# Layer 0 of a hybrid trunk: scale tiles loaded ahead of the shifts, half of the shifts taken as rows by VectorE

## The chip, the cores and the metric

The kernel runs on one core of a Trainium2 chip. The metric is the device time of one launch in microseconds. The engines are PE (TensorE, with its weight loads as PEld), DVE (VectorE), ACT (ScalarE), POOL (GpSimd) and SP (SyncE, which issues nearly all the DMAs here).

## The reference

A trunk of two layers runs over 128 context tokens and 512 latent tokens, 640 columns in all (`T`), with a width of 2048 (`D`), which is 16 tiles of 128 (`KT`). Context and latent tokens have a conditioning vector each (`c_ctx`, `c`), so every modulation is wanted twice. Cut to what matters:

```
shift, scale, gate = silu(cond) @ ada_w[l] + ada_b[l]          # three vectors of 2048
h = rms_norm(x, norm_g[l]) * (1 + scale) + shift
# layer 0 (even): qa ka va | qb kb vb rb | gp = h @ w_in        # rb: 32 rank columns, gp: 2048
y = concat(window_attention(...), gated_linear_attention(...)) * silu(gp)
# layer 1 (odd): neighbourhood attention | spatial-gating MLP, also * silu(gp)
x = x + gate * (y @ w_out[l])
```

After the two layers a final norm follows. Keys, values and scan states of the context are outputs too.

## The kernel before, in words

**Layout and projections.** Activations lie with the features on the partitions: 16 tiles of 128 x 640. Each projection (a "chunk" of 128 output features) runs over the 16 k-tiles in `mm_k` (L385), in two halves of 320 columns (`HT`). For fp32 accuracy each product is three matmuls: high part by high part, low part of the activation (`actl`, in the code `al`) by the high part of the weight, and high part of the activation (`acth`, `ah`) by the low part of the weight. One k of one chunk is so six matmuls. Weights come as `wraw` and are split by ACT (`whi`) and POOL (`wlo`); in the start the splits are called `suhi` and `sulo`.

**Modulation in a projection.** `act_mod` multiplies x by `A` = (1 + scale) * norm_g for one k-tile, and splits it. The norm's own factor (`rstd`) is applied when a sum leaves its bank. The shift can't be added there, so `ah` and `al` carry two more columns, the shift for context and for latent tokens; the first half of a chunk then has 322 columns, and those two come out as a bias. A chunk's third field in `add` says whether it takes these columns.

**The start (`start`).** Nothing of layer 0 can run before its scale and shift are there. `ada_w` of layer 0 comes as 16 tiles (f), each of 256 columns (128 of shift, 128 of scale) in four DMAs of 512 KB, through a ring of `NR` = 7 buffers (`Y` and `more`), beside three buffers for the tiles of x. For each quarter four fp32 matmuls of 32x256 run on four column groups of PE (L1311); ACT copies the sum, two matmuls with a selector (`sel`) turn it into columns, DVE makes `A` and the shift, and `act_mod` makes the tile. Two chunks (`LEAD`) follow tile by tile; the other six of the first eight (`FIRST`: six gates, the rank columns `w_rb` and the first query chunk) run in `WINDOWS` of k-tiles, each window summed into `YB` by DVE, the shift columns into `part_b`. The last window (k 12 to 15) is done behind the start by `finish`.

**Vectors that are taken as rows.** The gate vector of layer 0 and shift and scale of layer 1 are not made on PE. `ada_task` loads rows of the transposed weights (128 features x 512), and DVE multiplies each with the broadcast `silu(cond)` and sums along the row: one reduction for each of the two conditions, each with a read-out of the sum, into `part`. The jobs run one after another: `g0` (16 tiles), then `1` (32 tiles, shift first and scale behind it within each piece of 512 columns). They form a low-priority task (`self.low`) that yields to other work.

**Who sets the order.** A planner, `Pace`, keeps a modelled clock for each engine (`self.now`, `tick`) while the program is emitted, and each engine's order is what it emits. Chunks, evacuations, loads and the low task are emitted when the planner thinks them ready; loads go through SP's queue in the order of `dma`. A `need(flag)` keeps emission at a point until the flag is set: `need("ada_1")` (L2257) stands ahead of the handover from layer 0 to layer 1. The evacuation of an output pair makes two tiles of layer 1's x (bank times gate plus x, `OUT0` is their order); the handover scales these tiles by the new `A` and splits them while the last output pairs are still on PE, and PE's first chunks of layer 1 go k by k behind it.

## Time and profile before

| | |
|---|---|
| three runs | 2129.94, 2124.6, 2125.88 us; median 2125.88 us |
| profiled execution | 2124.6 us, of which the traced span is 2122.5 us |
| granted clock of PE, mean | 0.995 |
| busy share of the span | PE 97%, DVE 65%, POOL 52%, ACT 45% |
| DMA | 330.66 MB, mean 156 GB/s; 374 and 405 GB/s in the first two slices of 53 us |
| instructions | PE 14104, DVE 3235, ACT 2138, POOL 946 |

The busy share of PE counts pipelined matmuls whose ends are modelled, so 97% says that PE hardly ever waits, not that each of its matmuls is as short as it can be. Averages over the span say little about the two places that the change touches, the first 190 us and the end of layer 0 near 1040 us; both are read from stretches, waits and single instructions. In the rows a buffer is named by the program: `bank` is a PSUM bank, `adas` the four row buffers of `ada_task`, `more` and `Y` in the first 120 us the ring of modulation tiles.

### The profile page before, as it was taken

How to read it: one execution, taken by the hardware profiler on the slowest of the kernel's cores; microseconds unless marked ns; L12 is line 12 of the kernel's file. 1: busy time of each engine (PE TensorE's matmuls, PEld its weight loads, DVE VectorE, ACT ScalarE, POOL GpSimd, SP SyncE). 2: the span in 40 equal slices, each digit the busy share in tenths (PEclk: the TensorE clock that was granted, in tenths of full speed). 3: DMA queues.
4: the chain of work that ended last, by engine and by line, in shares of the span. 5: the costliest groups of instructions: out<-in, count | busy, mean ns of one | idle time of the engine just before them, and what ended most of it. 6: DMA issues, size and time to landing. Idle time of an engine off the chain costs nothing.

```text
span 2122.5 us, 39172 instructions
## 1 busy us (share of the span) xinstructions
PE 2064.9 (97%) x14104; PEld 1995.1 (94%) x14104; DVE 1378.1 (65%) x3235; ACT 945.2 (45%) x2138; POOL 1113.5 (52%) x946
## 2 busy tenths in 40 slices
PE   7999999999999999999999999999999999999996
PEld 4799999999989999999999999999999999999995
DVE  2437776777777875898766888777454444465335
ACT  3424444343333444543464444444444544454443
POOL 4333333223223223788665666555655577767883
PEclk9999999999999999999999999999999999999998
DMA  9925432345445335476843455443322344363337
GB/s 374 405 104 161 131 110 98 105 126 173 145 151 167 119 115 160 150 237 221 288 130 105 135 169 159 148 147 119 99 75 94 107 137 130 110 223 128 127 96 251
DMA packets 185283, 330.66 MB, mean 156 GB/s; under 512 B 20032, under 2 KB 69248, under 8 KB 185088
## 3 DMA queue, kind: packets, MB, share of 16 engines
q1 hardware_dynamic: 183616, 326.60, 46.9%
q8 instruction: 110, 1.80, 0.3%
q10 hardware_dynamic: 1472, 1.56, 0.2%
q14 instruction: 85, 0.70, 0.1%
HBM read 293.59 MB, written 31.87 MB: 153 GB/s over the span
## 4 chain that ended last, share of the span: by engine, by line
PE 86%; DVE 4%; DMA 3%; POOL 2%; ACT 2%; issue 2%; SPq 1%; ACTq 0%; DVEq 0%; POOLq 0%
PE bank L385 82%; PE bank L390 2%; POOL wlo L212 2%; PE bank L1311 1%; DVE arena L212 1%; DVE Y L212 1%; DVE adas L212 1%; DMA adas<-ada 1%; DMA wraw<-w_even 1%; SPq L418 1%; ACT whi L212 1%; POOL arena L212 0%; ACT arena L212 0%; DVE bank L212 0%; POOL actl L212 0%
## 5 line engine op out<-in xcount | busy, mean ns | idle before, releaser
L385 PE MATMUL bank<-acth,whi 128*128 128x320 f32 (+1 forms) x3296 | 1011.1, 318 | 7.4 <-DVE arena L212 2.8
L385 PE MATMUL bank<-actl,whi 128*128 128x320 f32 (+1 forms) x3296 | 985.8, 310 | 3.5 <-POOL actl L212 2.0
L385 PE MATMUL bank<-acth,wlo 128*128 128x320 f32 (+1 forms) x3296 | 985.9, 310 | 3.3 <-POOL wlo L212 3.2
L212 POOL TENSOR_TENSOR wlo<-wraw,whi 128x512 fp32r<-128x512 f32 (+1 forms) x449 | 571.4, 1284 | 646.8 <-ACT whi L212 565.2
L385 PEld LDWEIGHTS bank<-acth,whi 128*128 128x128 f32 x3296 | 611.5, 188 | 21.3 <-issue 4.9
L385 PEld LDWEIGHTS bank<-actl,whi 128*128 128x128 f32 x3296 | 611.5, 188 | 6.7 <-DMA actl<-bl_dram 2.8
L385 PEld LDWEIGHTS bank<-acth,wlo 128*128 128x128 f32 x3296 | 611.6, 188 | 5.2 <-POOL wlo L212 5.1
L212 POOL TENSOR_TENSOR wlo<-rs,whi 128x384 fp32r<-128x384 f32 x370 | 407.4, 1118 | 192.9 <-ACT whi L212 151.3
L212 ACT ACTIVATE whi<-wraw 128x512 fp32r<-128x512 f32 (+1 forms) x457 | 260.9, 588 | 148.6 <-PE bank L385 104.4
L385 PE MATMUL bank<-eh,whi 128*128 128x322 f32 (+1 forms) x666 | 209.4, 314 | 0.1
L385 PE MATMUL bank<-eh,wlo 128*128 128x322 f32 (+1 forms) x666 | 207.0, 311 | 1.7 <-POOL wlo L212 1.7
L385 PE MATMUL bank<-el,whi 128*128 128x322 f32 (+1 forms) x666 | 207.1, 311 | 0.0
L212 ACT ACTIVATE whi<-rs 128x384 fp32r<-128x384 f32 x370 | 181.6, 514 | 43.8 <-PE bank L385 35.3
L212 DVE CUSTOM_DVE_ANT_0 adas<-adas,bank,partg 128x256 bf16<-128x256 f32 (+1 forms) x320 | 178.4, 557 | 13.1 <-ACT bank L212 5.7
L212 DVE CUSTOM_DVE_ANT_0 adas<-adas,bank,part 128x512 bf16<-128x512 f32 x192 | 143.0, 745 | 18.2 <-ACT bank L212 6.9
L212 DVE TENSOR_TENSOR wraw<-rs 128x768 f32<-128x768 f32 x74 | 95.0, 1283 | 81.9 <-POOL wlo L212 49.8
L212 ACT ACTIVATE arena<-arena,bc 128x512 f32<-128x512 f32 (+4 forms) x211 | 106.0, 527 | 92.1 <-DVE arena L212 89.1
L212 DVE TENSOR_TENSOR bank<-bank,sums 128x320 f32<-128x320 f32 (+1 forms) x148 | 71.7, 495 | 100.7 <-PE bank L385 62.3
L385 PEld LDWEIGHTS bank<-eh,wlo 128*128 128x128 f32 x666 | 125.3, 188 | 2.8 <-POOL wlo L212 2.8
L385 PEld LDWEIGHTS bank<-eh,whi 128*128 128x128 f32 x666 | 125.7, 189 | 0.6 <-ACT whi L212 0.4
L385 PEld LDWEIGHTS bank<-el,whi 128*128 128x128 f32 x666 | 125.9, 189 | 0.0
L212 ACT ACTIVATE arena<-Y 128x320 f32<-128x320 f32 (+1 forms) x76 | 39.0, 513 | 154.7 <-DVE Y L212 127.0
(194 smaller groups left out, 2242.9 us busy)
## 6 DMA issues: line engine op xcount, KB each, us to landing
wraw<-w_even SPq DMA_DIRECT2D x176, 256.0 KB, 3.2
adas<-ada_g SPq DMA_DIRECT2D x128, 256.0 KB, 3.6
adas<-ada SPq DMA_DIRECT2D x128, 256.0 KB, 3.8
rs<-w_odd SPq DMA_DIRECT2D x50, 384.0 KB, 3.3
wraw<-w_odd SPq DMA_DIRECT2D x74, 256.0 KB, 3.6
more<-ada SPq DMA_DIRECT2D x36, 512.0 KB, 8.2
wraw<-w_out SPq DMA_DIRECT2D x64, 256.0 KB, 3.9
Y<-ada SPq DMA_DIRECT2D x28, 512.0 KB, 7.6
```

Source lines behind the costliest of these rows:

```text
L212: return f(*args, **kw)
L385: self.nc.tensor.matmul(out, lhsT, rhs, start=start, stop=stop, **kw)
L390: self.nc.tensor.transpose(out, in_, self.ident[:k, :k])
L418: self.nc.sync.dma_start(out, in_)
L1311: nc.tensor.matmul(o, c, w[:, j, :], start=(q == 0), stop=(q == 3))
```

## The change

Modulation of layer 0 is cut anew. `ada0` holds 24 tiles of 128 columns: first the 16 scale tiles, then the last eight shift tiles (`BOTH`), each in two DMAs of 512 KB. An activation tile needs only its scale, so it can be made ahead of the shifts. The first eight shift tiles are taken as rows (`shifts`): DVE reduces `ada_s0` against `silu(cond)`, which PE broadcasts into two banks by products with a one-hot matrix. The finished shift is written as columns into `ah` and `al`, and as rows into DRAM (`shift_s`).

The six gates of the start (`FIRST` is now 6) run before the shift is there, so they do without shift columns: 320 columns in place of 322, in windows of 2, 2, 4 and 8 k-tiles, summed in `yt(8 + c)`. What their shift columns would have given comes later as rows: a new job `b0` stands first in `ada_task`, which reduces the gates' weights (`gateT`) against the shift rows, and `gates0` then applies `rstd` (POOL) and SiLU with that bias (ACT). The rank chunk and the first query chunk become ordinary chunks behind the start. `finish`, with its last window, goes away, and `able` may take a window out of turn.

On **PE** the program begins so. `bank_71` holds the modulation sums, `bank_72` what the selector makes of them, `bank_67` to `bank_70` the first chunks. Before:

```order
L1311 MATMUL bank_71<-Y,cond_111 32x256 x12
L1311 MATMUL bank_71<-more_115,cond_111 32x256 x4
L385 MATMUL bank_72<-small,adas 128x2 x2
L1311 MATMUL bank_71<-more_115,cond_111 32x256 x8
L385 MATMUL bank_67<-acth,suhi_179 128x322
L385 MATMUL bank_68<-acth,suhi_179 128x320
L385 MATMUL bank_67<-actl,suhi_179 128x322
```

After:

```order
L1317 MATMUL bank_71<-Y,cond_112 32x128 x16
L386 MATMUL bank_72<-small,adas 128x2
L1317 MATMUL bank_71<-Y,cond_112 32x128 x8
L1317 MATMUL bank_71<-more_116,cond_112 32x128 x8
L386 MATMUL bank_67<-acth,suhi_156 128x320
L386 MATMUL bank_68<-acth,suhi_156 128x320
```

A tile is now 16 matmuls of 128 columns and one selector product, where it was 16 of 256 columns and two products; the first projection stands behind two tiles' worth of these matmuls, where it stood behind one and a half.

On **SP** the loads that stand at the same place are these. `wraw<-w_even` are weights of the first chunks, `Y<-xT` tiles of x. Before:

```order
L418 DMA Y<-ada 128x1024 x3
L418 DMA more_115<-ada 128x1024
L418 DMA Y<-xT 128x640
L418 DMA more_115<-ada 128x1024 x3
L418 DMA Y<-xT 128x640 x2
L418 DMA wraw<-w_even 128x512 x4
```

After, the first rows, and the place where the row loads come in (`raw` are their buffers, `ada_s` the transposed shift columns):

```order
L420 DMA Y<-ada 128x1024 x2
L420 DMA Y<-xT 128x640
L420 DMA wraw<-w_even 128x512
L420 DMA Y<-ada 128x1024
L420 DMA more_116<-ada 128x1024
```
```order
L420 DMA wraw<-w_even 128x512
L420 DMA raw_290<-crow_s 2x512
L420 DMA raw_291<-ada_s 128x512
L420 DMA raw_292<-ada_s 128x512
L420 DMA raw_293<-ada_s 128x512
L420 DMA raw_294<-ada_s 128x512
L420 DMA wraw<-w_even 128x512
L420 DMA Y<-ada 128x1024
```

The first weight load moved from behind seven pieces and three tiles of x to behind two pieces and one tile; row loads now stand among the scale pieces.

On **DVE**, at the end of layer 0, an `ISA` row is a reduction (two inputs) or its read-out (one), `bank_71` and `bank_67` or `bank_69` hold an output pair, and `A_95<-part` begins the scale of layer 1. Before:

```order
L212 ISA adas,part_103<-adas,bank_74,part_103 128x512
L212 ISA part_103 128x1
L212 TENSOR_TENSOR bank_71<-bank_71,sums_7739 128x320
L212 TENSOR_TENSOR bank_69<-bank_69,sums_7739 128x320
L212 SCALAR_TENSOR_TENSOR Y<-bank_69,G_96,arena_7743 128x128
L212 SCALAR_TENSOR_TENSOR Y<-bank_69,G_96,arena_7743 128x192
L212 SCALAR_TENSOR_TENSOR Y<-bank_71,G_96,arena_7743 128x320
L212 TENSOR_TENSOR A_95<-part_103,b_92 128x16
L212 TENSOR_TENSOR A_95<-A_95,small 128x16
```

After, where the line of dots stands for 22 more pairs of a reduction and its read-out, in two alternating banks:

```order
L213 TENSOR_TENSOR bank_71<-bank_71,sums_7907 128x320
L213 TENSOR_TENSOR bank_67<-bank_67,sums_7907 128x320
L213 SCALAR_TENSOR_TENSOR Y<-bank_67,G_96,arena_7911 128x128
L213 SCALAR_TENSOR_TENSOR Y<-bank_67,G_96,arena_7911 128x192
L213 SCALAR_TENSOR_TENSOR Y<-bank_71,G_96,arena_7911 128x320
L213 ISA adas,part_104<-adas,bank_73,part_104 128x512
L213 ISA part_104 128x1
...
L213 TENSOR_TENSOR A_95<-part_104,b_92 128x16
L213 TENSOR_TENSOR A_95<-A_95,small 128x16
```

Before, the last reduction stood ahead of this output pair's evacuation; now 24 reductions stand between the evacuation and `A_95`. The evacuation of the next output pair stands behind the whole scaling of layer 1's first tiles in both programs, and PE's first pair of layer 1 writes the banks of that output pair.

The core of the diff:

```diff
-WINDOWS = ((0, 2), (2, 2), (4, 4), (8, 4))
+WINDOWS = ((0, 2), (2, 2), (4, 4), (8, 8))
...
-LEAD, FIRST = 2, 8
+LEAD, FIRST = 1, 6
+BOTH = 8
...
+    lags0, room0, rows_at, pace0, NRAW, NRING = (0.2,) * 5, 1.2, 20.0, 0.4, 6, 6
...
+                    src = self.d["shift_s" if name == "b0" else "crow_s"]
+                    todo.append((fit, src[c : c + m, cs].partition_broadcast(128), bank[c : c + m]))
...
             def load(j):
-                if j < 4 * KT:
-                    self.dma(ring[j % NR], d["ada0"][j // 4, :, 4 * (j % 4) : 4 * (j % 4) + 4, :])
+                if j < 2 * (KT + BOTH):
+                    self.dma(ring[j % NR], d["ada0"][j])
...
             def tiles():
-                for f in range(KT):
-                    for q in range(4):
-                        w = ring[(4 * f + q) % NR]
+                for i in range(KT + BOTH):
+                    for q in range(2):
+                        w = ring[(2 * i + q) % NR].rearrange("p (a b) -> p a b", b=128)
                         yield from self.until(w)
-                        for j in range(4):
-                            o, c = pm[32 * j : 32 * j + 32, 0:256], cond[:, 4 * q + j, :]
-                            self.pe(0.15, o, c, w[:, j, :])
-                            nc.tensor.matmul(o, c, w[:, j, :], start=(q == 0), stop=(q == 3))
-                        load(4 * f + q + NR)
-                        if q % 2:
-                            yield
+                        for j in range(8):
+                            g = 32 * (j % 4)
+                            o, c = pm[g : g + 32, 0:128], cond[:, 8 * q + j, :]
+                            self.pe(0.075, o, c, w[:, j, :])
+                            nc.tensor.matmul(o, c, w[:, j, :], start=(q == 0 and j < 4), stop=(q == 1 and j >= 4))
+                        load(2 * i + q + NR)
+                        yield
                     r = rows.next()
-                    nc.scalar.activation(r, pm[:, 0:256], AF.Copy)
+                    nc.scalar.activation(r, pm[:, 0:128], AF.Copy)
                     yield from self.until(r)
                     p = pcol.next()
-                    self.mm(p[:, 0:2], r[:, 128:256], self.sel)
-                    self.mm(p[:, 2:4], r[:, 0:128], self.sel)
-                    nc.vector.tensor_scalar(
-                        self.A[0][:, f, :], p[:, 0:2], self.b1[:, 0, f : f + 1], self.ng[:, 0, f : f + 1], ALU.add, ALU.mult
-                    )
-                    sh = self.s("sh", 2)
-                    nc.vector.tensor_scalar(sh, p[:, 2:4], self.adab[:, 0, f : f + 1], None, ALU.add)
+                    self.mm(p, r, self.sel)
+                    f = i if i < KT else i - BOTH
+                    x = self.adab[:, 0, f : f + 1]
+                    if i >= KT:
+                        nc.vector.tensor_scalar(self.sh0[:, :, f], p, x, None, ALU.add)
+                        continue
+                    x, g = self.b1[:, 0, f : f + 1], self.ng[:, 0, f : f + 1]
+                    nc.vector.tensor_scalar(self.A[0][:, f, :], p, x, g, ALU.add, ALU.mult)
                     yield from self.wait(f"sq{f}")
                     self.act_mod(0, f, xs[f % NX], 0, T)
-                    nc.scalar.activation(self.ah[:, f, 0:2], sh, AF.Copy)
-                    nc.vector.tensor_tensor(self.al[:, f, 0:2], sh, self.ah[:, f, 0:2].bitcast(F32), ALU.subtract)
                     load_x(f + NX)
                     self.flags.add(f"act{f}")
+                self.flags.add("tiles")
...
+            def shifts():
+                raws = [self.t(su, [128, PIECE], "raw", bufs=self.NRAW) for _ in range(self.NRAW)]
+                junk = self.t(su, [128, PIECE // 2], "junk").bitcast(BF16)
+                one = self.t(su, [2, 2, 128], "one", F32R)
+                hi, lo = (self.t(su, [2, PIECE], x, F32R) for x in ("chi", "clo"))
+                nc.vector.tensor_copy(one, self.ident[0:2, 0:2, None].to_broadcast([2, 2, 128]))
+                pc = self.banks[2:4]
...
+                for q in range(4):
+                    cs = slice(PIECE * q, PIECE * q + PIECE)
+                    todo += [(None, d["crow_s"][:, cs]), *((f, d["ada_s0"][f, :, cs]) for f in range(NB))]
+                def load(i):
+                    if i < len(todo):
+                        x = raws[i % len(raws)]
+                        self.dma(x[0:2, :] if todo[i][0] is None else x, todo[i][1])
...
+                for i, (f, _) in enumerate(todo):
+                    raw = raws[i % len(raws)]
+                    if f is None:
...
+                        for c, p in enumerate(pc):
+                            self.mm(p, one[:, c, :], hi, stop=False)
+                            self.mm(p, one[:, c, :], lo, start=False)
+                        continue
...
+                        nc.vector.tensor_tensor_reduce(junk, raw, p, 1.0, acc if i > NB else 0.0, ALU.mult, ALU.add, acc)
+                        yield self.pace0
...
+                yield from self.wait("tiles")
+                self.shifts(self.ah[:, :, 0:2], self.al[:, :, 0:2], self.sh0.rearrange("p c f -> p f c"))
+                self.flags.add("shift0")
...
+                self.dma(d["shift_s"].rearrange("a (b c) -> (a b) c", c=128), crow)
+                self.flags.add("rows0")
...
-                M, y = self.chunks[c][1], self.ysum(c)
-                pieces = [(y[:M, 0:HT], pw[:M, 2 : 2 + HT]), (self.part_b[:M, c, :], pw[:M, 0:2])]
-                if half:
-                    pieces = [(y[:M, HT:T], pw[:M, 0:HT])]
-                for y, p in pieces:
-                    if k0 == 0:
-                        nc.scalar.activation(y, p, AF.Copy)
-                    else:
-                        nc.vector.tensor_tensor(y, y, p, ALU.add)
-            for j in range(4):
+                    if k % 2:
+                        self.tick(2)
+                y = self.yt(8 + c)[:, HT * half : HT * half + HT]
+                if k0 == 0:
+                    nc.scalar.activation(y, pw[:, 0:HT], AF.Copy)
+                else:
+                    nc.vector.tensor_tensor(y, y, pw[:, 0:HT], ALU.add)
...
+            def able():
+                for i, (c, k, n, half) in enumerate(todo[:6]):
+                    if all(x[0::3] != (c, half) for x in todo[:i]) and ready(c, *range(k, k + n)):
+                        return todo[i]
+            for j in range(NR):
                 load(j)
-            load_x(0)
-            for j in range(4, NR):
-                load(j)
-            load_x(1)
-            load_x(2)
+                if j % 2 and j < 2 * NX:
+                    load_x(j // 2)
+                    self.wload()
+            for f in range(NR // 2, NX):
+                load_x(f)
...
+            self.low, self.room, self.lags = [self.rows_at, shifts()], self.room0, self.lags0
...
+    def gates0(self):
         nc = self.nc
-        M, y = self.chunks[c][1], self.ysum(c)
-        def evac(pa, pb):
-            add = lambda p, x: nc.vector.tensor_tensor(p, p, x, ALU.add)
-            if pa is not None:
-                add(pa[:M, 2 : 2 + HT], y[:M, 0:HT])
-                add(pa[:M, 0:2], self.part_b[:M, c, :])
-            if pb is not None:
-                add(pb[:M, 0:HT], y[:M, HT:T])
-            self.chunks[c][4](pa, pb)
-        self.units(c, 12, evac)
+        for a, b in ((0, 2), (2, FIRST)):
+            if a:
+                yield from self.wait("gla_elem1")
+            for i in range(a, b):
+                nc.gpsimd.tensor_tensor(self.yt(8 + i), self.yt(8 + i), self.rstd, ALU.mult)
+                yield
+            yield from self.until(self.yt(7 + b))
+            for i in range(a, b):
+                y, z = self.yt(8 + i), self.part["b0"][:, i, :]
+                self.act(y[:, 0:NCTX], y[:, 0:NCTX], AF.Silu, bias=z[:, 0:1])
+                self.act(y[:, NCTX:T], y[:, NCTX:T], AF.Silu, bias=z[:, 1:2])
+                self.flags.add(f"gp{8 + i}")
...
-        for i in range(8, 14):
-            gp_first(i)
+        for i in range(FIRST):
+            add(wE[36 + i], 128, False, None, None)
...
                 self.ada_task(
                     [
+                        ("b0", d["gateT"], FIRST, 512, lambda: self.spawn(self.gates0()), 0.4),
                         ("g0", d["ada_g0"], 16, 512, lambda: self.fin_gate(0, self.part["g0"]), 0.4),
                         ("1", d["ada_1"], 32, 512, lambda: self.fin_scale(1, self.part["1"][:, 16:32, :]), 0.4),
...
+    x = np.concatenate([s[:, :, 16:32], s[:, :, 16 - BOTH : 16]], 2)
+    o["ada0"] = x.reshape(2, 8, 128, KT + BOTH, 128).transpose(3, 0, 2, 1, 4).reshape(-1, 128, 1024)
     awT = aw.transpose(0, 2, 1).reshape(2, 48, 128, D)
+    o["ada_s0"] = awT[0, 0 : 16 - BOTH]
...
+    o["gateT"] = we[:, 3616 + 1024 : 3616 + 1024 + 128 * FIRST].T.reshape(FIRST, 128, D)
```

More of the change, by code (lines that the diff above doesn't have):

```diff
@@ L70, in span @@
     def span(self, ap):
-        if ap.space == bass.MemoryType.DRAM and ap.name not in (SPILL, YSP, *KEEP):
+        if ap.space == bass.MemoryType.DRAM and ap.name not in (SPILL, YSP, SHIFTS, *KEEP):
             return None
@@ L536, in unit @@
             self.plain.append((c, k))
-        for k in (0, 4, 8, 12):
+        for k, n in WINDOWS:
             for c in range(FIRST):
-                unit(c, k)
+                for j in range(k, k + n):
+                    if j % 4 == 0:
+                        unit(c, j)
         last = None
@@ L1285, in load_x @@
                     self.flags.add(f"xs{f}")
-            banks = [[self.pj(), self.pj()], [self.pj(), self.pj()]]
+            banks = [[self.pj(), self.pj()] for _ in range(LEAD)]
             pm, pw = self.sm(), self.sm()
-            pws = Ring([self.sm(), self.sm()])
-            pcol = Ring([pw[:, 400 + 4 * i : 404 + 4 * i] for i in range(4)])
+            pws = Ring([self.sm() for _ in range(2)])
+            pcol = Ring([pw[:, 400 + 2 * i : 402 + 2 * i] for i in range(4)])
             def squares():
@@ L1336, in ready @@
             def ready(c, *ks):
[L1337 removed]
                 return (
[L1339 removed]
+                    all((c, k - k % 4, 0) in self.parts for k in ks)
                     and all(f"act{k}" in self.flags for k in ks)
[L1341 removed]
+                    and self.left(*self.parts[c, ks[0] - ks[0] % 4, 0], *(a[:, k, 2:] for k in ks for a in (self.ah, self.al))) <= 0.0
                 )
```

82 lines of the change are left out of this document (48 added, 34 removed).

## The prediction

> **What bounds the kernel now.** I read the page first, then 20 us stretches of the first 140 us, then the chain of waits, and last the two places where the order of instructions changes most. The page:
>
> ```profile
> PE 2064.9 (97%) x14104; PEld 1995.1 (94%) x14104; DVE 1378.1 (65%) x3235; ACT 945.2 (45%) x2138; POOL 1113.5 (52%) x946
> PE 86%; DVE 4%; DMA 3%; POOL 2%; ACT 2%; issue 2%; SPq 1%; ACTq 0%; DVEq 0%; POOLq 0%
> ```
>
> PE carries 86% of the chain that ended last. So an edit pays only where PE waits, or where it takes matmuls away. The stretches (columns: length, then busy us and count of PE, PEld, DVE, ACT, POOL; granted clock, DMA share, GB/s):
>
> ```profile
> 0.00:20.00 20.00, 9.03 (x58) 3.79 (x59) 2.28 (x7) 6.30 (x12) 2.93 (x10) 1.00 0.90 327
> 20.00:40.00 20.00, 15.34 (x120) 9.80 (x119) 6.23 (x10) 8.45 (x20) 14.20 (x11) 0.83 1.03 402
> 40.00:60.00 20.00, 20.00 (x190) 14.78 (x183) 4.75 (x15) 8.33 (x21) 5.96 (x4) 1.00 1.03 404
> 100.00:120.00 20.00, 20.00 (x176) 15.99 (x176) 9.06 (x23) 9.35 (x19) 10.30 (x8) 1.00 0.72 274
> 120.00:140.00 20.00, 18.63 (x127) 18.15 (x126) 8.28 (x21) 4.46 (x10) 4.92 (x5) 1.00 0.21 67
> GB/s 84 210 396 418 409 389 408 410 402 383 408 404 401 405 406 398 404 404 409 408 404 400 411 405 407 401 410 409 404 406 406 405 402 397 411 404 401 248 42 61
> ```
>
> DMA is full until about 113 us at 404 GB/s (last row: 3 us slices of the first 120 us), but PE is dense from 40 us on. So PE bounds the rest of this stage; its loss lies ahead of 40 us. The chain and PE's own rows price the work there:
>
> ```profile
> 50.07 0.57 PE bank L1311 x8
> 53.72 1.00 PE bank L1311 x16
> 116.26 1.99 PE bank L385 x12
> 121.95 43.18 PE bank L385 x292
> 166.30 33.76 PE bank L385 x227
> ```
> ```profile
> 32.70 0.56 PE L385 MATMUL bank<-actl,suhi 128*128 128x322 f32 x2 [1.74 <-DVE actl L212]
> 36.47 0.74 PE L385 MATMUL bank<-actl,suhi 128*128 128x322 f32 x2
> 50.97 0.46 PE L385 MATMUL bank<-actl,suhi 128*128 128x322 f32 x2
> 53.22 0.50 PE L385 MATMUL bank<-small,adas 128*128 128x2 f32 x4
> ```
>
> A projection matmul costs 148 ns (43.18 us / 292). After a wait PE runs at half rate: 0.74 us for two at 36.47 us, 0.46 us later. A run of 8 modulation records costs 0.57 us, of 16 1.00 us: 0.215 us for four records and 0.14 us for each change of run.
>
> **Start of layer 0, before.** Gates, rank and first query chunk take 768 projection matmuls. At 166.30 us, 144 are left (six chunks, four k, six each): the block ends at 166.30 + 144 x 0.148 = 187.6 us.
>
> **Start, after.** Modulation is 384 instructions of 128 columns (768 records) in place of 256 of 256 (512 records). Their price is not in the trace; the nearest rows are these:
>
> ```profile
> L1311 PEld LDWEIGHTS bank<-more,cond x288: 106/109/178, 10.5 to 115.2; 128*32 128x32 f32 x144
> L1311 PE MATMUL bank<-more,cond x288: 379/379/637, 10.5 to 115.5; 128*32 128x256 f32 x144
> ```
>
> Four records run side by side on four column groups, every 0.215 us. With half the columns that is 0.107 us, which a weight load of 106 ns still fits. Bounds: 27 ns a record (streaming halves) to 54 ns (nothing halves). I take 27 ns, since the four start together and so issue is no limit: 768 x 0.027 = 20.5, 48 runs x 0.14 = 6.7, 27 us or 1.13 us a tile; before it was 512 x 0.054 + some 45 x 0.14 = 34 us.
>
> When do tiles land? The first slices moved 2.07 MB in 9 us, so data come at 3.9 us + MB / 0.404, and 0.8 us more to land. In SP's order tile 3 is whole at 6.46 MB (20.7 us) and the last at 42.45 MB (109.8 us). With tile 3 and the matmuls ahead of it PE stands at about 25 us, 36 projection matmuls done. To the last tile it has 384 more (56.8), 20 tiles (22.6), 40 selector records at 0.125 (5), 8 broadcasts of 512 columns at 0.24 (1.9), norm sums (1.5): 113 us, just behind DMA's 109.8. Then 156 projection matmuls and the last broadcasts (24.2) end the gates at 137; rank and query chunks (192, 28.4) at 165.6. Before, PE lost 3.7 us at 118.25 and 1.2 us at 165.13 to DVE; I carry over 4. End: 169.6, **18 us earlier**. Bounds: 22 us with no such waits, and 0 with 54 ns a record.
>
> What hides the rest: the last shift row lands at 45.86 MB, 118.2 us. DVE's 64 reductions cost:
>
> ```profile
> L212 DVE CUSTOM_DVE_ANT_0 adas<-adas,bank,part x192: 731/748/750, 654.9 to 1043.1; 128x512 bf16<-128x512 f32 x192
> L212 DVE DVE_READ_ACCUMULATOR2_ANT part<- x256: 76/83/89, 519.8 to 1043.7; 128x1 f32 x128
> L212 DVE CUSTOM_DVE_ANT_0 adas<-adas,bank x128: 406/681/690, 173.1 to 1168.8; 128x512 bf16<-128x512 f32 x96, 128x256 bf16<-128x256 f32 x32
> ```
>
> 16 x 0.76 + 48 x 0.83 = 52 us, on an engine busy 31 of 100 us in the five rows above; the shift columns are ready near 122 us, 15 us ahead of the rank chunk at 137. If that cover goes, the rank chunk waits for it. SP's new row loads wait for DVE to free a buffer, and the weight and tile loads queue behind them; six scale pieces in flight cover that. The two columns less per first-half matmul, one activation in place of 16 two-column ones, the smaller copies and the rows' round trip through DRAM go off the path: nothing.
>
> **The gates' columns as rows.** 48 reductions and read-outs (12 x 0.76 + 36 x 0.83 = 39 us of DVE), 32 DMAs of 256 KB, eight bank copies on ACT, four more table loads, six POOL products. Taken away: 12 DVE additions and 12 scalings of about 0.49 us. DVE and PE stand there so:
>
> ```profile
> 160.00:200.00 40.00, 38.82 (x263) 38.56 (x262) 29.57 (x79) 20.00 (x46) 14.09 (x13) 1.00 0.49 145
> PE bank L385 <- DVE arena L212: 3.9, 6, 2.0
> ```
>
> From 100 to 900 us PE waits 3.9 us for this DVE group. An evacuation that falls behind a reduction comes 0.8 us late. I add 0.5 us (0 to 4); the gates themselves are needed only at their products with attention and GLA.
>
> **The end of layer 0.** What DVE gains in work it gives back here. Both low-priority jobs follow the new one, and layer 1's scale comes from the last. The DVE order shows it: ahead of `A<-part` there are now 24 reductions and read-outs that stood ahead of the evacuation before. DVE's and ACT's rows now:
>
> ```profile
> 1040.69 0.75 DVE L212 CUSTOM_DVE_ANT_0 adas<-adas,bank,part 128x512 bf16<-128x512 f32 x1 [2.69 <-DMA adas<-ada]
> 1042.27 0.75 DVE L212 CUSTOM_DVE_ANT_0 adas<-adas,bank,part 128x512 bf16<-128x512 f32 x1
> 1043.06 0.75 DVE L212 CUSTOM_DVE_ANT_0 adas<-adas,bank,part 128x512 bf16<-128x512 f32 x1
> 1044.66 1.13 DVE L212 SCALAR_TENSOR_TENSOR Y<-bank,G,arena 128x128 f32<-128x128 f32 x3
> 1045.71 0.17 DVE L212 TENSOR_TENSOR A<-part,b 128x16 f32<-128x16 f32 x1
> 1069.56 1.14 DVE L212 SCALAR_TENSOR_TENSOR Y<-bank,G,arena 128x128 f32<-128x128 f32 x3
> 1072.21 1.14 DVE L212 SCALAR_TENSOR_TENSOR Y<-bank,G,arena 128x128 f32<-128x128 f32 x3 [1.51 <-PE bank L385]
> ```
> ```profile
> 1049.10 1.00 ACT L212 ACTIVATE Y<-Y,A 128x128 f32<-128x128 f32 x2
> ```
> ```profile
> 1000.00:1040.00 40.00, 24.11 (x64) 0.00 (x0) 1.00 0.72 227
> PE bank L385 <- DVE Y L212: 2.2, 1, 2.2
> PE bank L385 <- POOL actl L212: 2.0, 2, 1.1
> PE bank L385 <- POOL wlo L212: 1.3, 2, 0.7
> ```
>
> Reductions follow each other every 0.79 us: 24 take 19 us, at the pace of the stretch to 1040 us (32 in 40 us, first row) 30. I take 19 plus one half of a DMA wait like that of 2.69 us: 20.3. The scaling of layer 1 then starts at 1069.4 instead of 1049.10. From there to the evacuation at 1069.56 DVE and ACT need 20.5 us, in the same order and with as many weight splits: 1089.9. PE ends the last output pair at 1072.2 and writes layer 1's first pair into the banks which that evacuation frees: it **waits 17.7 us**. ACT's weight splits stand behind the late scale too, so part of the wait may fall earlier, inside the output pair; the sum stays. A restart at half rate for 4.5 us (32.70 to past 36.47 us above) adds 2.2; of the 3.3 us that PE waits for POOL behind it, I count 2.9 as covered: +17 us. Bounds: +12 if loads never wait and ACT is quick, +26 at 1.25 us a reduction.
>
> [...]
>
> **Sum.** The profiled execution took 2124.6 us (span 2122.5), the median of the runs is 2125.88. 2124.6 - 18 + 0.5 + 17 = **2124 us**, no change by the bound of 0.3% (6.4 us), which is about what a measurement of this kernel can tell from none.
>
> **Rivals.**
> 1. The handover hurts less: scaling needs less than the 20.5 us because ACT has done its other work meanwhile, and loads never stall the reductions. For: ACT idles there; against: each k needs ACT then DVE in turn. +8 instead of +17: 2115 us. Chance 0.22.
> 2. The start gains 25 us, since the waits on DVE go with the two-column additions: 2117 us. Against: DVE gets 64 reductions in one queue with the evacuations. Chance 0.14.
> 3. Slower: reductions at the end of layer 0 come every 1.25 us as in the stretch to 1040 us, because SP's loads queue behind activation reloads. The handover costs 26: 2133 us. It decides above 1.2 us a reduction. Chance 0.13.
> 4. Slower: 128-column records cost 54 ns. The last tile's matmuls then end near 130 us and the start gains nothing: 2142 us. Chance 0.1.
> 5. The change doesn't do what it says: row loads hold up the scale pieces in SP's queue, activations come 5 us late, the gain is 13: 2129 us, still no change. Chance 0.06.
>
> The sum as forecast has 0.35. Faster 0.36 (1 and 2), within 0.3% 0.41, slower 0.23. The range reaches over rivals 1 to 3 and part of 4: 2109 to 2139; the forecast's own is 2119.5 to 2132.
>
> **What would show it.** Right: a run of 16 records in about 0.57 us; the query chunk's last matmul near 169 us; a PE wait of over 10 us between 1030 and 1085 us, released by DVE or by ACT's splits, with 24 reductions just ahead of `A<-part`. Wrong: no such wait, or PE idle around 100 to 140 us behind modulation loads or reductions.

## The result: 1.1% slower, and the profile after

The changed kernel takes 2152.61 us (median of four runs, 2150.45 to 2153.35), the kernel before 2127.05 us beside it: a ratio of 1.011, with an interval from 1.0097 to 1.0123. The forecast was 2124 us in a range to 2139. The profiled execution has a span of 2148.7 us at a granted clock of 0.988 (before 2122.5 us and 0.995).

The page, the waits of PE over the whole span (what waited, what released it; us in all, times, longest), and stretches as in the prediction:

```profile
PE 2070.7 (96%) x14361; PEld 2009.8 (94%) x14361; DVE 1430.8 (67%) x3391; ACT 952.7 (44%) x2128; POOL 1128.3 (53%) x952
```
```profile
PE bank L386 <- ACT whi L213: 16.1, 1, 16.1
PE bank L386 <- DVE Y L213: 3.8, 1, 3.8
```
```profile
0.00:20.00 20.00, 9.53 (x111) 6.72 (x112) 4.43 (x9) 8.33 (x17) 6.46 (x12) 0.96 0.84 323
20.00:40.00 20.00, 20.00 (x214) 17.63 (x214) 10.54 (x12) 12.53 (x29) 12.23 (x9) 0.87 1.03 397
200.00:1000.00 800.00, 782.77 (x5264) 762.39 (x5264) 611.22 (x1373) 352.21 (x763) 329.62 (x255) 1.00 0.46 148
1050.00:1100.00 50.00, 31.72 (x189) 30.29 (x188) 35.06 (x91) 21.10 (x45) 17.02 (x14) 0.80 0.56 183
```

PE is now dense from 20 us on, as meant. The loss is seen in the last row: 18 of 50 us idle, at a mean clock of 0.80. The same 800 us of layer 0 before:

```profile
200.00:1000.00 800.00, 787.75 (x5320) 768.68 (x5319) 612.95 (x1366) 346.99 (x755) 316.56 (x250) 1.00 0.46 148
```

PE is idle there for 17.2 us in place of 12.3. The waits of PE from 190 to 1040 us, before and after, show for what:

```profile
PE bank L390 <- DVE arena L212: 4.5, 4, 1.6
PE bank L385 <- DVE arena L212: 3.9, 6, 2.0
PE bank L385 <- POOL wlo L212: 1.7, 4, 0.7
```
```profile
PE bank L386 <- POOL wlo L213: 6.7, 8, 1.4
PE bank L386 <- DVE arena L213: 4.4, 6, 2.0
PE bank L391 <- DVE arena L213: 3.6, 4, 1.6
```

The waits for DVE did not grow (8.0 us after 8.4); those for POOL's weight splits did, by 5 us.

To say when the start pays I count the matmuls of `actl` (one to every three, in each kernel): 256 are six gates, rank and first query chunk over 16 k. After, up to 177.5 us (groups by form):

```profile
L386 PE MATMUL bank<-actl,whi 128*128 128x320 f32 x160 | 49.5, 309 | 0.0
L386 PE MATMUL bank<-actl,suhi 128*128 128x320 f32 x48 | 13.5, 337 | 0.0
L386 PE MATMUL bank<-actl,whi 128*128 128x322 f32 x16 | 5.0, 311 | 0.0
L386 PE MATMUL bank<-actl,whi 128*96 128x322 f32 x16 | 5.0, 310 | 0.0
L386 PE MATMUL bank<-actl,whi 128*96 128x320 f32 x16 | 4.9, 309 | 0.0
```

That is 256. Before, the 256th came at 187.5 us (forecast 187.6): the start **gains 10 us**, not 18. Farther on the matmuls of `el`, another buffer of low parts, are counted too (108 up to the end of layer 0). By the 1880th, in the last output pair of layer 0 (before 1055.8 us, after 1056.9), the lead is gone: it was 7.8 us at the 600th (before 372.9 us), 6.6 at the 1500th (881.2), 2.0 at the 1700th (971.4) and 0.7 at the 1850th (1039.0).

At the end of layer 0, DVE, ACT and PE of the changed kernel show:

```profile
1045.52 1.14 DVE L213 SCALAR_TENSOR_TENSOR Y<-bank,G,arena 128x128 f32<-128x128 f32 x3
1046.57 0.74 DVE L213 CUSTOM_DVE_ANT_0 adas<-adas,bank,part 128x512 bf16<-128x512 f32 x1
1054.63 0.75 DVE L213 CUSTOM_DVE_ANT_0 adas<-adas,bank,part 128x512 bf16<-128x512 f32 x1 [1.77 <-DMA adas<-ada]
1069.13 0.17 DVE L213 TENSOR_TENSOR A<-part,b 128x16 f32<-128x16 f32 x1
```
```profile
1048.12 0.61 ACT L213 ACTIVATE whi<-wraw 128x512 fp32r<-128x512 f32 x1
1070.02 0.23 ACT L1075 ACTIVATE acth<-part 128x32 fp32r<-128x32 f32 x1 [21.29 <-DVE part L213]
1072.88 0.61 ACT L213 ACTIVATE whi<-wraw 128x512 fp32r<-128x512 f32 x1
```
```profile
1046.25 0.64 PE L386 MATMUL bank<-acth,whi 128*128 128x320 f32 x1 [3.80 <-DVE Y L213]
1049.35 0.46 PE L386 MATMUL bank<-acth,whi 128*128 128x320 f32 x2
1073.55 0.90 PE L386 MATMUL bank<-acth,whi 128*128 128x320 f32 x2 [16.07 <-ACT whi L213]
1079.46 0.73 PE L386 MATMUL bank<-actl,whi 128*128 128x320 f32 x2
1080.33 0.46 PE L386 MATMUL bank<-acth,whi 128*128 128x320 f32 x2
```

From 1046.57 to 1069.13 DVE makes the 24 reductions (22.6 us). ACT's next weight split is queued behind the activation that needs their result, 21.29 us late. PE stops for 16.07 us inside the output pair, for want of that split, and runs at half rate until past 1079.46.

### The profile page after: what moved, and what is told of

Its sections match the earlier page's. It is cut to its first block, busy times and chain, and to the rows that moved or that the text cites. A ratio compares the mean times of both kernels' runs of the same rounds, so it can differ in the third digit from the quotient of the medians.

```text
span 2148.7 us, 40029 instructions
## 1 busy us (share of the span) xinstructions
PE 2070.7 (96%) x14361; PEld 2009.8 (94%) x14361; DVE 1430.8 (67%) x3391; ACT 952.7 (44%) x2128; POOL 1128.3 (53%) x952
## 5 line engine op out<-in xcount | busy, mean ns | idle before, releaser
L386 PE MATMUL bank<-acth,whi 128*128 128x320 f32 (+2 forms) x3320 | 1024.2, 319 | 25.3 <-ACT whi L213 16.1
L386 PE MATMUL bank<-acth,wlo 128*128 128x320 f32 (+2 forms) x3320 | 997.5, 311 | 7.3 <-POOL wlo L213 7.2
L386 PE MATMUL bank<-actl,whi 128*128 128x320 f32 (+2 forms) x3320 | 996.8, 311 | 4.2 <-DMA actl<-bl_dram 2.4
L386 PEld LDWEIGHTS bank<-acth,whi 128*128 128x128 f32 (+1 forms) x3320 | 619.3, 189 | 37.2 <-ACT whi L213 16.8
L386 PEld LDWEIGHTS bank<-acth,wlo 128*128 128x128 f32 (+1 forms) x3320 | 619.1, 189 | 10.7 <-POOL wlo L213 10.4
L386 PEld LDWEIGHTS bank<-actl,whi 128*128 128x128 f32 (+1 forms) x3320 | 619.5, 189 | 7.1 <-DMA actl<-bl_dram 3.5
L213 POOL TENSOR_TENSOR wlo<-rs,whi 128x384 fp32r<-128x384 f32 x370 | 415.9, 1142 | 173.3 <-ACT whi L213 140.2
L213 DVE CUSTOM_DVE_ANT_0 adas<-adas,bank,part 128x512 bf16<-128x512 f32 x192 | 143.1, 745 | 17.7 <-DMA adas<-ada 12.9
```

The lines of the kernel that those rows point to most:

```text
L213: return f(*args, **kw)
L386: self.nc.tensor.matmul(out, lhsT, rhs, start=start, stop=stop, **kw)
```

## The experiments

Each edits the changed kernel unless it says otherwise. The ratios are to the kernel before. `b0` is the new job of 48 reductions for the gates' shift part.

### The start: what a run of modulation matmuls costs

**Longer runs.** Both pieces of a tile are awaited and then 32 records issued in a row:

```diff
-for q in range(2):
-    w = ring[(2 * i + q) % NR]...
-    yield from self.until(w)
+ws = [ring[(2 * i + q) % NR]... for q in range(2)]
+for w in ws:
+    yield from self.until(w)
```

> The changed kernel with both pieces of a modulation tile in one run of 32 records (24 runs instead of 48). Theory C (change of run): a run of 16 costs PE 0.76 us from the last projection matmul to the next, of which 0.43 are the records (27 ns each) and 0.33 the change to another kind of matmul and back; half the runs save 24 x 0.33 = 8 us, about 2145 us. Rival D: PE would wait for the second piece from DMA instead, or VectorE sets the pace of the start: within 2 us of the changed kernel.

It took 2155.6 us (1.0125, 1.0104 to 1.0146). PE's rows, a run of the changed kernel first, then one of this (start and span in us):

```profile
87.34 0.31 PE L386 MATMUL bank<-acth,wlo 128*128 128x320 f32 x1
87.58 0.64 PE L1317 MATMUL bank<-Y,cond 128*32 128x128 f32 x16
88.15 0.57 PE L386 MATMUL bank<-acth,suhi 128*128 128x320 f32 x2
```
```profile
70.18 0.31 PE L386 MATMUL bank<-acth,wlo 128*128 128x320 f32 x1
70.42 1.08 PE L1319 MATMUL bank<-Y,cond 128*32 128x128 f32 x32
71.43 0.56 PE L386 MATMUL bank<-acth,suhi 128*128 128x320 f32 x2
```

From start to start a run of 16 holds PE for 0.57 us and one of 32 for 1.01: 16 records more cost 0.44, so **27 ns a record**, as forecast. What is left of the 0.57 is 0.13. The projection ahead takes 0.24 to the next start where one costs 0.148 (0.09 more), and the two behind it span 0.57 where two cost 0.46 (0.10 more). So a run costs 0.33 us beyond its records; the forecast had 0.14, from lines of the chain that cut these edges off. The longer runs gained nothing here: the 256th `actl` matmul came at 178.3 us. The rows have 24 runs in place of 43 (five pairs of the 48 stand back to back), which at 0.33 us would save 6 us; 4.4 of them went into idle time of PE, 16.7 us of the first 140 in place of 12.3. The rest is not settled.

**No rows.** All 16 shift tiles on PE again: `BOTH = 16`.

> The changed kernel with all 16 shift tiles on PE (BOTH = 16): no rows of the shift in the start, so 64 reductions less on VectorE there and 256 more fp32 matmul records on PE in 16 runs, 8 x (2 x 0.76 + 0.07) = 12.7 us of PE. Theory Q (the end of layer 0 is set by the scale of layer 1, which comes out of the queue of reductions, not by PE): the 256th k-step of the projections ends near 190 us instead of 177.5, but the scale comes at 1060 to 1069 us as before, the wait just shrinks by what PE is later: 2148 to 2154 us, the same. Rival A (times add up): 2152 + 13 = 2165 us.

2159.57 us (1.0142, 1.0118 to 1.0165). The 256th `actl` matmul came at 185.1 us: eight tiles cost 7.6 us. The expectation that the scale of layer 1 would stay where it was did not hold: it came at 1078.5 us, 9.4 later, about as much as PE was later (8 us at the 1880th). So the row queue seems to move with PE's progress; this one run does not show why.

**Half the columns in the kernel before.** Only the scale half of each tile is loaded and multiplied; the shift is left out (the scale's sums stand in its place).

```diff
-o, c = pm[32 * j : 32 * j + 32, 0:256], cond[:, 4 * q + j, :]
+o, c = pm[32 * j : 32 * j + 32, 128:256], cond[:, 4 * q + j, :]
```

> The kernel before with the scale half of each modulation tile alone: 256 KB less per load (8.4 MB in all) and 128 columns in place of 256; the shift columns of layer 0 take the scale's sums, so the shift is left out. It gives the old kernel an earlier start with nothing put on VectorE. Loads end 20 us earlier, so the first 256 k-steps end near 167 us instead of 187.5, and the queue of reductions starts as much earlier. If a lead at 180 us is carried to the end as long as the queue has it too: about 2108 us. Rival P (GpSimd's splits and VectorE's chains set the pace up to 1040 us and take the lead back): 2119 us or more.

2114.98 us (0.9935, 0.9918 to 0.9952). The lead is 13.3 us at the 256th `actl` matmul (174.2 us), 8.7 at the 1880th and, by the two profiled executions (2115.5 and 2124.6 us), 9 at the end; the medians are 14 apart. So most of a lead at the start can be carried to the end; the changed kernel loses its own on the way.

**The gates' part on PE.** `b0` is replaced by 96 matmuls of 128 columns against the shift columns.

```diff
-("b0", d["gateT"], FIRST, 512, lambda: self.spawn(self.gates0()), 0.4),
+nc.tensor.matmul(o, self.shc[:, 4 * q + j, :], raws[q][:, 128 * j : 128 * j + 128], ...)
```

> The changed kernel with b0's work on PE: 24 loads of 256 KB of gate weights as they lie, 96 fp32 matmuls of 32x128 in four column groups in 12 runs of 8, a copy and a selector product for each of the six gates, in place of 48 reductions. Theory Q: VectorE is rid of 40 us, A is ready before PE wants it and the wait of 16 us goes; PE pays 12 x (0.22 + 0.33) + 6 selector products, 7 us: about 2129 us, no slower than before. Rival L (loads): the wait hangs on the loads of the row buffers, of which as good as all stay: 2145 us or more.

2150.79 us (1.0108, 1.0093 to 1.0123), with the 256th at 189.1 us: 11.6 later than in the changed kernel. The scale comes at 1056.2 us, and PE waits nowhere for longer than 1.2 us at the handover. The rows of one run:

```profile
158.21 0.64 PE L1482 MATMUL bank<-adas,shc 128*32 128x128 f32 x16
158.78 0.39 PE L386 MATMUL bank<-acth,whi 128*96 128x322 f32 x1
```

Twelve such runs at 0.57 us and 0.19 of edges are 9.1 us of the 11.6. What the handover gives back is lost on the way to it as well: against the kernel before, this one stands 1.6 us behind at the 256th and 20.5 behind at the 1850th, so it loses 19 us beside layer 0, where the changed kernel loses 9. So taking the reductions off DVE did not keep the lead there; why is not shown.

### The handover

These rows are the scale of layer 1 (`A`, first and last start of two additions) after, without `b0`, and with half of it:

```profile
L213 DVE TENSOR_TENSOR A<-part,b x2: 169/170/172, 1069.1 to 1069.4; 128x16 f32<-128x16 f32 x2
```
```profile
L213 DVE TENSOR_TENSOR A<-part,b x2: 170/536/903, 1005.8 to 1006.9; 128x16 f32<-128x16 f32 x2
```
```profile
L213 DVE TENSOR_TENSOR A<-part,b x2: 168/527/886, 1044.5 to 1044.8; 128x16 f32<-128x16 f32 x2
```

**Without `b0`.** The gates go without their shift part, which is zero.

```diff
-("b0", d["gateT"], FIRST, 512, lambda: self.spawn(self.gates0()), 0.4),
+nc.vector.memset(self.part["b0"], 0.0)
+self.spawn(self.gates0())
```

> The changed kernel without the job b0: its 48 reductions and 32 loads are gone, so the six gates get no part from the shift. Theory Q (queue): the 23 us at the handover, and the 4 to 5 us that PE loses between 200 and 1000 us, come from b0's 40 us of VectorE work ahead of the scale of layer 1. Then the scale is ready near 1046 us minus the start's gain, the PE wait of 16 us is gone, and only the start's gain of 9 us is left: about 2118 us. Rival S (start): the new start itself leaves work behind it (row loads, later rank and query chunks) that makes the low-priority jobs late; then the wait stays and the time is above 2140 us.

2129.44 us (1.0001, 0.9991 to 1.001). The long wait is gone, 23 us with it. But it is no faster than the kernel before.

**The same, with `gates0` 65 us later**, where `b0` would have let it go:

```diff
+self.spawn(self.gates0(), delay=65.0)
```

> As the first run without job b0 (the six gates get no part from the shift), but their product with rstd and their SiLU start 65 us later by the planner's clock, about where the changed kernel has them; the first run had them at once, and PE lost 5.9 us to VectorE at one transpose there. Theory Q: the start's gain of 9 to 13 us is then left over nearly whole: about 2120 us, faster than before. Rival P (pace of others): what PE gains at the start it loses again to GpSimd's weight splits and to VectorE between 200 and 1030 us, since those set the pace there: 2127 us or more, no gain at all.

2124.86 us (0.999, 0.9981 to 0.9998). The second row above is this kernel's.

**Half of `b0`:** two of its four pieces of columns, so 24 reductions.

```diff
+for q in range(2 if name == "b0" else D // n):
```

> The changed kernel with half of job b0: two of the four pieces of 512 columns, 24 reductions (the gates get half of their part from the shift). A stood at 1069 us with 48 reductions and at 1011 us with none; by theory Q it stands at about 1040 us now, which is when PE gets there, so a wait of 0 to 4 us: about 2130 us, that is nearly all of the loss is gone with half of the reductions. Rival N (no threshold: each reduction costs PE its own time wherever it stands): half way, 2141 us.

2128.68 us (1.0003, 0.9993 to 1.0013): `A` 24.6 us earlier than after (third row above), PE's longest wait for ACT's split 3.1 us, and 23.9 us less in all. So the whole loss against the kernel before comes with the last 24 reductions.

**The job alone in the kernel before:** 48 reductions of other rows, not used.

```diff
+("b0", d["ada_g0"], 6, 512, lambda: None, 0.4),
```

> The kernel before with a job of b0's size set ahead of the other two: 48 reductions over rows of the gate weights, whose sums nobody reads. Theory Q: the first reduction into part of layer 1 comes 42 us later, PE waits some 18 us more at the end of layer 0 and runs at half rate behind it: 2127 + 23 + 4, about 2152 us, with the old start. Rival S: no wait, at most 2132 us.

2173.2 us (1.020, 1.0178 to 1.0223). `A` comes 48.7 us later, and PE waits 27.9:

```profile
L212 DVE TENSOR_TENSOR A<-part,b x2: 169/170/171, 1094.4 to 1094.7; 128x16 f32<-128x16 f32 x2
```
```profile
PE bank L385 <- ACT whi L212: 30.4, 2, 27.9
```

**The loads of `b0` alone**, no reduction (its sums are zero):

```diff
+if name != "b0":
     nc.vector.tensor_tensor_reduce(
```

> The changed kernel with all loads and copies of job b0 but without its 48 reductions (the gates get no part from the shift). Theory Q (VectorE's time): as without b0, 2125 to 2130 us. Rival L (the 32 loads of 256 KB in SP's queue make weights and later rows late): near the changed kernel, 2145 us or more.

2143.58 us (1.007, 1.0056 to 1.0084), PE waiting 7.0 us. The row buffers (`adas`) in this kernel and in the changed one; the third busy time is DVE's:

```profile
150.00:200.00 50.00, 0.00 (x0) 0.00 (x0) 0.00 (x0) 6.00 (x10) 0.00 (x0) 1.00 0.81 261
```
```profile
150.00:200.00 50.00, 0.00 (x0) 0.00 (x0) 27.62 (x38) 4.61 (x8) 0.00 (x0) 1.00 0.74 232
```
```profile
L213 DVE TENSOR_TENSOR A<-part,b x2: 167/170/172, 1058.4 to 1058.7; 128x16 f32<-128x16 f32 x2
```

The first reduction of the next job, `g0`, starts at 202.6 us; without `b0` it starts at 157.0. So the 32 loads (24 of weights, 8 of shift rows) hold the queue of row work for 45 us by themselves, 1.4 us each, and `A` comes at 1058.4. DVE's time is not the only price of a row job: its loads take turns too, here for 18.7 of the 27.8 us between the kernel with late `gates0` and the changed one.

**`b0` sooner:** DVE gives it more room and no pause.

```diff
-self.room = self.rooms[0]
+self.room = 3.0
-("b0", ..., lambda: self.spawn(self.gates0()), 0.4),
+("b0", ..., self.b0_done, 0.0),
```

> The changed kernel with b0 pressed: no pace between its reductions and room 3.0 instead of 0.3 for the planner while it runs (what VectorE may be behind before a reduction is held back). b0 took 73 us for its 48 reductions (158 to 231 us), 1.5 us each against 0.79 back to back. If the planner's holding back makes the queue late: b0 takes 50 us or less, the scale of layer 1 comes some 20 us earlier (1050 us), evacuations between 158 and 210 us come late by up to 5 us: about 2137 us. Rival L: the row loads (3 in flight, 3.6 us each, 1.2 us a load) and what follows in the queue set the rate: scale within 8 us of 1069 us, 2145 to 2157 us.

2155.68 us (1.0124, 1.0105 to 1.0144). Its read-outs end 23 us sooner, yet `A` comes at 1073.0, not earlier:

```profile
L213 DVE DVE_READ_ACCUMULATOR2_ANT partb<- x48: 72/83/84, 157.9 to 230.9; 128x1 f32 x48
```
```profile
L213 DVE DVE_READ_ACCUMULATOR2_ANT partb<- x48: 78/83/85, 156.1 to 208.0; 128x1 f32 x48
```

The first row is the changed kernel. What is gained by 208 us is gone by the handover.

**Scale first.** The 16 scale tiles of layer 1 get a job of their own ahead of the shift tiles, and what needs the shift waits for that:

```diff
-("1", d["ada_1"], 32, 512, ...fin_scale...),
+("1s", d["ada_1"][16:32], 16, 512, ...fin_scale...),
+("1", d["ada_1"][0:16], 16, 512, lambda: None, 0.4),
```

> The changed kernel with the rows of layer 1 in another order: all 16 scale tiles first, then the 16 shift tiles (before, both went through each piece of 512 columns). The same reductions; the handover waits for the scale alone, the fold and the first products that take shift columns wait for the rest. Theory Q: A is ready long before the last output pairs, so the wait of 16 us inside the output pair goes; the 24 late reductions then lie beside the last output pair (some 14 us of PE work after it) and a rest of 5 to 8 us of waiting for the shift stays: about 2136 us. Rival L: the reductions are late because their loads are late (12.9 us of VectorE waits for them), and the end of all of them sets the time whatever their order: 2148 us or more.

2152.32 us (1.0106, 1.0083 to 1.0129). `A` is there at 914.8 us, and PE waits all the same, 17.8 us, now for the shift columns, whose reductions end at 1096:

```profile
PE bank L386 <- ACT acth L1079: 17.8, 1, 17.8
```

Here the total of the queue counts, not its order.

### Where the lead goes, and whether the whole version can keep it

**Reductions held back in linear attention**, without `b0` (the kernel with late `gates0`, and one number changed):

```diff
-rooms = (0.3, 1.5, 0.8)
+rooms = (-0.1, 1.5, 0.8)
```

> As the run without b0 and with the later gates, but while the gated linear attention runs VectorE's reductions are held back more: the planner's room is -0.1 us instead of 0.3. There the run before it lost 5.9 us at one wait of PE for a scan result of VectorE (300 to 400 us), and the 10 us that the start had gained ended as 4. If reductions in front of the attention's own VectorE chain took the lead, that wait goes, the scale is still early enough (it had 40 us to spare), and the lead arrives: about 2118 us, faster than before. Rival: PE then meets the next chain some microseconds later: 2124 us or more.

2118.04 us (0.9959, 0.9946 to 0.9971). Late `gates0` alone lost 8 us of its lead near 386 us, at this wait and the half rate behind it (PE):

```profile
386.23 0.48 PE L391 MATMUL bank<-ident,Y 128*128 128x128 f32 x1 [5.89 <-DVE Y L213]
386.77 0.47 PE L386 MATMUL bank<-actl,whi 128*128 128x320 f32 x1
390.51 0.31 PE L386 MATMUL bank<-actl,whi 128*128 128x322 f32 x1
```

Held back, the wait is gone, and the stretch of 800 us reads:

```profile
200.00:1000.00 800.00, 788.11 (x5306) 768.75 (x5305) 607.28 (x1359) 356.34 (x771) 330.63 (x261) 1.00 0.46 146
```

PE idles for 11.9 us in place of 17.7 without it; the lead is 10.6 us at the start and 8.7 at the 1880th low-part matmul (1047.1 us). At the end it is 10 by the medians and 4 by the profiled executions (2120.79 and 2124.6 us). By the medians this is what the new start is worth when the gates' shift part is left out.

**More room with `b0` complete.** Three versions of the changed kernel give reductions more of DVE: the first throughout, the other two while `b0` runs, behind linear attention, and in the second half.

```diff
-rooms = (0.3, 1.5, 0.8)
+rooms = (0.6, 1.5, 1.6)        # first
+rooms = (0.3, 1.5, 1.6)        # second and third
+self.room = 0.4                # second, while b0 runs (third 0.6)
+if "gla_elem2" in self.flags and self.room == self.rooms[0]:
+    self.room = 0.8            # second (third 0.7)
```

> The changed kernel, complete, with more room for the reductions in the first half of layer 0 (0.6 instead of 0.3 us that VectorE may be behind, and 1.6 instead of 0.8 in the second half). If the place of 48 more reductions is the whole trouble, some can be bought earlier for short waits of PE: the scale comes some 10 us earlier relative to PE, the wait of 16 us shrinks by as much, and waits of 10 us in all appear between 200 and 850 us: about 2145 us, little better. Rival: VectorE's chains in the attention then hold up PE more than the end gains: above 2152 us.

> The changed kernel, complete, with the room for reductions set by stage: 0.4 while b0 runs, 0.3 to the linear attention's second chain, 0.8 behind it, 1.6 in the second half of layer 0. The run with 0.6 throughout and 1.6 took 16 us off the changed kernel. If reductions cost least where PE does not wait for VectorE's chains (behind the linear attention, not in it), this takes some 4 to 6 us more: 2131 us, near the kernel before. Rival: nothing more to gain, 2136 us.

> As the run beside it, with 0.6 while b0 runs and 0.7 behind the linear attention's second chain: the scale then comes early enough for PE not to wait for it, for waits of about 4 us more ahead of it. Same forecast, 2131 us; if what counts is only the wait for the scale it is the better of the two.

2136.4 us (1.0043, 1.0027 to 1.0058), 2137.16 (1.004, 1.0025 to 1.0055) and 2134.32 (1.0028, 1.0018 to 1.0039). The third has its scale at 1050.8 us:

```profile
L213 DVE TENSOR_TENSOR A<-part,b x2: 167/520/874, 1050.8 to 1051.1; 128x16 f32<-128x16 f32 x2
```
```profile
PE bank L386 <- DVE Y L213: 2.9, 1, 2.9
PE bank L386 <- ACT whi L213: 2.5, 1, 2.5
```

The long wait is gone and 18 us with it, but the 1880th low-part matmul comes at 1061.3 us (1056.9 in the changed kernel), and PE idles for 22.9 us from 200 to 1000 us in place of 17.2. That the reductions now delay evacuations is likely, but not shown. It is the fastest of the complete versions and still does not beat the kernel before.

## Why the prediction failed, step by step

From before to after the medians differ by 25.6 us, the two profiled spans by 26.2. Leads and stretches are counted in these two executions:

| step | forecast | measured |
|---|---|---|
| start, to the 256th `actl` matmul | -18 | -10 |
| from there to 1039 us, beside layer 0 | +0.5 | +9 |
| handover, wait | +15 | +17.6 (3.80 + 16.07 - 2.23) |
| handover, half rate | +2.2 | +4.4 (1.5 + 2.9) |
| handover, other waits | 0 | +1 |
| behind it | 0 | +3.6 |

- **Dense PE from 20 us, 27 ns a record:** held. Rival 4 (54 ns) fell, and so did rival 2 (25 us), although the waits on DVE that it wanted gone were gone: PE idles 0 us from 140 to 178. The start came nearest to rival 5 (13 us), but PE did not wait there for late activations.
- **"48 runs x 0.14" failed.** A run costs 0.33 us beyond its records, so the 43 runs in the rows cost 8 us more, and the start missed by 8. Lines of the chain of waits cut the edges off; starts of single rows show them. That the two agree so well is partly luck: the 4 us of waits that the sum carried over did not come (the 3.7 and 1.2 us there were pieces of the chain; PE idled for 1.37 and 1.18), and broadcasts, norm sums and the way to the first tiles took about as much more. The 0.8 us to land was my estimate, and no row shows it; by the page of the changed kernel a piece of 512 KB took 6.9 us from issue to landing (24 of them into `Y`, median; 7.6 before, 28 of them).
- **"I add 0.5 us (0 to 4)" failed.** Nine were lost, five of them as idle PE from 200 to 1000 us. I had taken the waits for DVE before as a measure of what more DVE work would cost. These did not grow; the waits for POOL's weight splits did, by 5 us. One more stop of 2.02 us (at 846.91 us) was followed by 3.4 us of half rate, some 1.5 us. What made the splits late stays open. The job alone cost the kernel before as much: with `b0` it was 3.7 us behind at the 256th and 13 at the 1850th. But without `b0`, with late `gates0`, 9 us went too, most of them at the one wait at 386 us, which the changed kernel does not have. Held-back reductions kept that lead, so where reductions stand matters in that kernel; for the changed kernel it is inferred.
- **"What DVE gains in work it gives back here" held.** 24 reductions before `A`, 22.6 us (forecast 20.3; 3.8 of them are waits for row loads, where 1.35 were forecast), `A` at 1069.1 us. The wait fell inside the output pair, behind ACT's queued split, as the prediction allowed. Rival 1 (+8) and rival 3 (1.25 us a reduction; it was 0.94) did not come. The whole handover cost 23 us against 17 forecast.
- **The restart was mis-sized.** At the handover two stops, not one, were followed by half rate, and behind the longer it lasted 6.45 us (a cost of 2.9). The 4.5 us of the forecast were misread too: between the two rows that it used, one at 33.09 us has 0.46 for two, full rate, and the rows show half rate from about 33.7 to 37.1 us, 3.4 us.
- **Behind it**, 3.6 us are not settled. Two go between 1772 and 1906 us of the kernel before, the rest behind 2040; PE idles 1.8 us more from 1772 us on, and a stretch of half rate at 2114 us costs about 1.5. All kernels with the new start lose 1.4 to 6.6 us there, those without `b0` too (1.7, 3.0 and 4.4), so `b0` is not needed for it. Nor was it tried to give `b0` buffers of its own, or another engine than DVE or PE.

The loss was missed because the gain of the start was counted nearly whole and its carrying on taken for granted; the danger that was named, at the handover, came with 23 us in place of 17.

## What to carry to other kernels

In this kernel, a low-priority queue that ends in a deadline cost little until its end met the deadline, and then nearly its full length: 24 reductions cost 4 us against none, and the next 24 cost 24 us. Before such work is added, read from the trace when its last result comes and when it is first needed; its loads count in the queue as well as its arithmetic. A lead won early is not yet time won: follow it along the program by counting one kind of matmul in both traces. Price a change between kinds of matmul from start to start of single rows, with the neighbours on both sides.

## What was not expected of the hardware

- Switching PE between a run of 32-column matmuls and 128x128 ones cost 0.33 us beyond the 27 ns a record (in the changed kernel, from the rows at 87.34, 87.58 and 88.15 us).
- Half rate behind a stop did not follow the length of the stop. In the changed kernel 3.4 us followed a stop of 2.02, 3.1 one of 3.80 and 6.45 one of 16.07; in the kernel before none followed 2.23 (at 1045.39 us; the next pairs of matmuls take 0.46 us). With late `gates0` some 4 us followed 5.89, with the job alone in the kernel before some 6 followed 27.90. In the traces of before and after a stretch of granted clock 0.50 is 3.41 us long or a whole multiple of it, the one at the end of the program left out (six around the 16 us stop, from 1059.60 to 1080.08 us). A stop shorter than such a stretch stood ahead of one: behind 2.02 us the clock was 0.50 from 847.97 to 851.38 us.

```profile
846.91 0.41 PE L386 MATMUL bank<-acth,whi 128*128 128x320 f32 x1 [2.02 <-DVE arena L213]
848.11 0.73 PE L386 MATMUL bank<-actl,whi 128*128 128x320 f32 x2
```

- Thirty-two row loads of 256 KB, issued as buffers came free, held the queue of row work for 45 us with no arithmetic behind them (the loads of `b0` alone: DVE 0.00 us on the row buffers from 150 to 200 us, where late `gates0` without `b0` has 27.90).
